# Attention output projection: the first two output blocks summed head by head inside the attention's steps, a third ahead of the last head's part

## The chip, the cores and the metric

The kernel runs on one core of one Trainium2 chip. The metric is the device time of one execution in microseconds (us); of a kernel that was run several times it is the median.

## What is computed

The program is a two-layer transformer block (first part) followed by a second block with a state-space branch and a latent-attention branch. Width 1024, 256 positions, batch 1. The change touches the attention of the first part's second layer and what follows it:

```python
q = rope(rms_norm((h @ w_q[j]).reshape(B, T, N_HEADS, HEAD_DIM), q_norm[j]), cos, sin).transpose(0, 2, 1, 3)
att = moba_attention(q, k_blocks, v_blocks, k_mean)         # 8 heads of 128; 256 positions are one block
y = att.transpose(0, 2, 1, 3).reshape(B, T, D) @ w_o[j]     # output projection, 1024 x 1024
x = x + (1.0 + g)[:, None, :] * y
h = modulate(rms_norm(x, norm_g[layer, 2]), sh, sc)         # input of the feed-forward network behind it
```

Since the sequence is one attention block, each head is a causal softmax attention of 256 queries over 256 keys. The output projection sums over all 8 heads: output block n (128 of the 1024 outputs) is the sum over heads k of `w_o[k, n]` (128 x 128) times head k's result (128 x 256).

## The kernel before

**Number format.** A float32 operand is split into a rounded high part and the rest (`hi` and `lo`, type fp32r). A product is hi*hi + lo*hi + hi*lo. `mm2` (lines 363 and 364) does that with two matmuls: the high weights against both halves of the activation side by side (512 columns), and the low weights against the high half (256 columns). `mm3` (line 356) does it with three of 256 columns.

**The weight stream.** All weights come as tiles of 128 x 1024 float32 (512 KB) in one fixed order, in three pools of 5 buffers (`wraw`, `whi`, `wlo`). SyncE's queue loads a tile (line 215), ScalarE casts it to `whi` (line 229), VectorE subtracts to get `wlo` (line 220). The stream keeps up to 4 split tiles ahead: `Stream.next()` first splits until 4 tiles are ahead, then hands out the oldest; `next(True)` ("hold") hands out the oldest and splits nothing. With `late`, the VectorE halves of new splits are queued in a list that the next call of `next` emits first; where the tile handed out is itself among the new ones, the whole list is emitted at once. An engine's instructions stand in the order in which the Python code emits them. The DMA that refills a raw buffer is emitted behind the VectorE half that frees it.

**The attention** (`attention`). The query projection (`proj_b`) comes first; it leaves three tiles of `w_o` split and waiting. Then a loop over `it` from 1 to 10 runs the heads as a pipeline. In step `it`: `s1a(it)` computes the scores (lines 879 to 882) and their maxima (VectorE, 884 to 889); `s1b(it-1)` the exponentials (ScalarE, line 896) and the division (VectorE, 898 and 900); `s2(it-2)` transposes the probabilities (line 907) and copies them (ScalarE, 909); `s3(it-3)` multiplies with the values (840, 841) and writes the head's result to `oo` (trace name `ohl`), high half by ScalarE (842), low half by VectorE (843). Scores end with head 7 in step 7; steps 8 to 10 only finish heads.

**The output projection** (`proj_a`). Eight output blocks n, one after the other. Each takes one weight tile (all 8 heads of that block): 8 pairs of matmuls on TensorE, one per head, into a PSUM bank with tag A or B in turn. Then `update` (line 558) adds the block, times the gate, to the residual `X` with two VectorE operations, ScalarE squares `X` for the next normalisation (lines 471, 473, 479), and GpSimd adds the squares (484). With each block, `next()` splits the tile four ahead, and a planner (`plan`, `tick`) lets out one of two waiting matrix-vector rows (`gemv`, VectorE, line 389). PSUM has 8 banks: tags A, B, C and D with two each. Tag C is free from step 5 on.

**Behind it.** `st_half` and `st_finish` sum the squares (line 500), take the power -0.5 on GpSimd (520) and spread the result by TensorE (526); `modulated` writes the next input `hhl` (533 to 538), and the next feed-forward network starts on TensorE with line 356.

Of the kernel before, what the change touches and what calls it, by code (L numbers as in the profile page):

```python
# [18 lines left out]
KB = 8  # L19
# [11 lines left out]
W_OUT = (1.2, 1.6, 1.5, 1.6)  # L31
KV_A = 97
AT_A, AT_Q, AT_O = 150, 0, 2
KV_W = [0] * 2 + [1] * 13
SLOTS = 135
CUTS = (0, 0.27, 0.27, 0.6)
# [214 lines left out]
class Kernel:  # L251
# [391 lines left out]
            self.flush()  # L643
            self.st_half(D, gap)

    def proj_a(self, a, evac, kb=KB, tiles=8, tags="AB", late=True, wide=0):
        hi = lo = None
        for n in range(tiles):
            p = self.ps(tags[n % len(tags)])
            mm, w = (self.mm2, 2 * T) if n < wide else (self.mm3, T)  # L650
            for k in range(kb):
                b = n * kb + k
                if b % 8 == 0:
                    hi, lo = self.next(late=late)
                mm(p[:, :w], hi, lo, b % 8, a[:, k], k == 0, k == kb - 1)
            evac(n, p[:, :w])
        self.los()
# [134 lines left out]
    def attention(self, hh, gate_fn, pre):  # L792
        nc, V = self.nc, self.nc.vector
        with self.tc.tile_pool(name="attn", bufs=1) as self.ap:
            self.rope_table(1, "q", 1.0)
            QT = self.ap.tile([128, 8, T], F32, name="QT")
            rq = self.ap.tile([128, 8, 2], F32, name="rq")
            self.shift(self.ap, 192)
            oo = self.ap.tile([128, 8, 2, T], F32R, name="ohl")
            pend = []  # L800

            def evac(nch, pp):
                while pend:
                    pend.pop(0)()
                if nch:
                    last_pp.extend(pp)
                    return
                stats(pp, nch)
                for th in range(2):
                    rope(pp[th], nch, th)  # L810

            def stats(pp, nch):
                for th in range(2):
                    self.qk_stats(pp[th], nch, th, rq)

            def rope(p, nch, th):
                m1 = self.qk_rope(p, nch, th, rq, "q")
                pend.append(lambda: self.qk_transpose(m1, QT, nch, th))
            last_pp = []
            S, P, PT = {}, {}, {}  # L820

            def rest():
                while pend:
                    pend.pop(0)()

            def s1a(h):
                S[h] = self.softmax_a(self.ps("D" if h < 2 else "A"), QT[:, h], self.KT[:, h], 0,
                                      lambda th: rq[:, h, th:th + 1], rq[:, h, :])

            def s1b(h):  # L830
                P[h] = self.softmax_b(*S.pop(h))

            def s2(h):
                PT[h] = self.p_transpose(P.pop(h))

            def s3(h):
                pt = PT.pop(h)
                po = self.ps("D")
                d = slice(h * 128, h * 128 + 128)
                nc.tensor.matmul(po[:, :256], self.VV[:, 0, d], pt[:, :256], start=True, stop=False)  # L840
                nc.tensor.matmul(po[:, 128:256], self.VV[:, 1, d], pt[:, 256:], start=False, stop=True)
                nc.scalar.copy(oo[:, h, 0], po[:, :T])
                V.tensor_sub(oo[:, h, 1], po[:, :T], oo[:, h, 0].bitcast(F32))

            mids = self.gemvs(AT_A, 152)
            first, mids, last = mids[:AT_Q], mids[AT_Q:len(mids) - AT_O], mids[len(mids) - AT_O:]
            self.plan(first, [0] * 3 + [1] * 3)
            self.proj_b(hh, 2, evac, hooks={HQ: rest, (1, 6): lambda: s1a(0)})
            self.drain()
            for it in range(1, 11):  # L850
                if it == 4:
                    rest()
                if it < 8:
                    s1a(it)
                if it - 1 < 8:
                    s1b(it - 1)
                if it == 1:
                    stats(last_pp, 1)
                if 0 <= it - 2 < 8:
                    s2(it - 2)  # L860
                if it < 3:
                    rope(last_pp[it - 1], 1, it - 1)
                if 0 <= it - 3 < 8:
                    s3(it - 3)
                if mids:
                    mids.pop(0)()
            g = gate_fn()
            self.st_begin(KB)

            self.plan(mids + last, [1] * len(mids + last))  # L870
            self.proj_a(oo, lambda n, p: self.update(n, p, g), wide=KB - 1)
            self.drain()
            self.pre = pre()
            self.st_half(D, "g11")
# [66 lines left out]
    def phase1(self):  # L941
# [12 lines left out]
        with ExitStack() as p1:  # L954
# [152 lines left out]
            for l in range(2):  # L1107
# [32 lines left out]
                if l == 0:  # L1140
# [5 lines left out]
                    self.modulated(rbs, self.pre, hh)  # L1146
                    self.plan(self.gemvs(KV_A, 104), KV_W, ssm[2], 16)
                    self.kv_project(hh)
# [800 lines left out]
```

## Time and profile before

| | |
|---|---|
| median of 3 runs | 1303.39 us |
| lowest and highest of the 3 | 1303.30 and 1306.41 us |
| the profiled execution | 1308.08 us |
| its span, first to last instruction | 1306.3 us |
| mean granted TensorE clock in the span | 0.987 of full |
| busy share of the span: TensorE, VectorE, ScalarE, GpSimd | 96%, 78%, 51%, 13% |
| attention's loop of steps, in the profiled execution | from 704.8 to 726.4 us |
| output projection | from 726.4 to about 748.9 us |

The trace is that of the profiled execution, one core. 1.8 us of its time lie outside its span. In the trace, a matmul's duration holds its way through the array, so neighbours overlap: the time that a matmul takes from the engine is read from start to start. A number in square brackets behind a row is the engine's idle time before it and what ended it. PEclk is the granted clock of TensorE: 1.00 is 2.4 GHz, 0.50 is 1.2 GHz.

### The profile page before, as it was taken

How to read it: one execution, taken by the hardware profiler on the slowest of the kernel's cores; microseconds unless marked ns; L12 is line 12 of the kernel's file. 1: busy time of each engine (PE TensorE's matmuls, PEld its weight loads, DVE VectorE, ACT ScalarE, POOL GpSimd, SP SyncE). 2: the span in 40 equal slices, each digit the busy share in tenths (PEclk: the TensorE clock that was granted, in tenths of full speed). 3: DMA queues.
4: the chain of work that ended last, by engine and by line, in shares of the span. 5: the costliest groups of instructions: out<-in, count | busy, mean ns of one | idle time of the engine just before them, and what ended most of it. 6: DMA issues, size and time to landing. Idle time of an engine off the chain costs nothing.

```text
span 1306.3 us, 25415 instructions
## 1 busy us (share of the span) xinstructions
PE 1258.7 (96%) x9870; PEld 1167.4 (89%) x9870; DVE 1015.6 (78%) x1768; ACT 669.4 (51%) x1170; POOL 165.3 (13%) x285
## 2 busy tenths in 40 slices
PE   7999999999999999999998999999999899989998
PEld 5999988899988779999886899998888888989997
DVE  6789896789999789999977777878853576537774
ACT  4455444555444665544447555444465855437443
POOL 1000011100002000121111201000210791100000
PEclk9999999899999999999999999999998999989999
DMA  9899996788899568998974478778655544764852
GB/s 365 297 344 386 335 369 237 251 310 259 274 326 332 203 256 299 312 324 301 360 279 145 129 237 268 265 258 282 223 195 172 156 130 124 226 202 143 292 191 81
DMA packets 119850, 331.14 MB, mean 253 GB/s; under 512 B 28273, under 2 KB 39409, under 8 KB 119666
## 3 DMA queue, kind: packets, MB, share of 16 engines
q1 hardware_dynamic: 119730, 329.52, 73.4%
q8 instruction: 77, 1.26, 0.4%
q14 instruction: 43, 0.35, 0.1%
HBM read 317.94 MB, written 10.49 MB: 251 GB/s over the span
## 4 chain that ended last, share of the span: by engine, by line
PE 71%; DVE 4%; ACT 4%; issue 2%; DMA 2%; POOL 1%; SPq 0%; DVEq 0%; ACTq 0%; POOLq 0%
PE psD L356 13%; PE psB L356 12%; PE psA L356 11%; PE psC L356 7%; PE psA L363 5%; PE psB L363 4%; PE psA L364 3%; PE psB L364 2%; DVE wlo L220 1%; PE psA L368 1%; PE psA L369 1%; PE psA L370 1%; PE psB L368 1%; PE psB L370 1%; PE psB L369 1%
## 5 line engine op out<-in xcount | busy, mean ns | idle before, releaser
L220 DVE TENSOR_TENSOR wlo<-wraw,whi 128x1024 fp32r<-128x1024 f32 x391 | 481.3, 1236 | 44.6 <-ACT whi L229 43.4
L229 ACT CAST whi<-wraw 128x1024 fp32r<-128x1024 f32 x391 | 403.1, 1049 | 94.5 <-ACT whi L229 32.7
L356 PE MATMUL psA<-hhl,whi 128*128 128x256 f32 x960 | 247.4, 283 | 4.7 <-ACT hhl L534 4.6
L356 PE MATMUL psB<-hhl,whi 128*128 128x256 f32 x976 | 248.4, 281 | 0.0
L356 PE MATMUL psD<-hhl,whi 128*128 128x256 f32 x1120 | 213.7, 283 | 0.4 <-ACT hhl L534 0.4
L356 PEld LDWEIGHTS psA<-hhl,whi 128*128 128x128 f32 x960 | 180.2, 189 | 7.9 <-ACT hhl L534 6.2
L356 PEld LDWEIGHTS psB<-hhl,whi 128*128 128x128 f32 x976 | 183.8, 190 | 0.0
L389 DVE SCALAR_TENSOR_TENSOR junk<-graw,cb 128x1024 bf16<-128x1024 f32 x146 | 179.3, 1228 | 5.5 <-DMA cb<-in_c 5.5
L356 PEld LDWEIGHTS psD<-hhl,whi 128*128 128x128 f32 x1120 | 178.6, 190 | 2.7 <-issue 1.8
L356 PE MATMUL psD<-hhl,wlo 128*128 128x256 f32 x560 | 157.2, 281 | 0.0
L356 PE MATMUL psB<-hhl,wlo 128*128 128x256 f32 x488 | 136.9, 281 | 0.0
L356 PE MATMUL psA<-hhl,wlo 128*128 128x256 f32 x480 | 134.9, 281 | 1.3 <-DVE wlo L220 1.3
L363 PE MATMUL psA<-shl,whi 128*128 128x512 f32 x352 | 123.8, 392 | 0.0
L356 PEld LDWEIGHTS psD<-hhl,wlo 128*128 128x128 f32 x560 | 106.3, 190 | 0.0
L364 PE MATMUL psA<-shl,wlo 128*128 128x256 f32 x352 | 99.2, 282 | 0.0
L356 PE MATMUL psC<-hhl,whi 128*128 128x256 f32 x480 | 93.4, 286 | 0.4 <-DVE hhl L1456 0.4
L356 PEld LDWEIGHTS psA<-hhl,wlo 128*128 128x128 f32 x480 | 91.2, 190 | 1.7 <-DVE wlo L220 1.7
L356 PEld LDWEIGHTS psB<-hhl,wlo 128*128 128x128 f32 x488 | 92.4, 189 | 0.0
L363 PE MATMUL psB<-shl,whi 128*128 128x512 f32 x264 | 92.2, 390 | 0.0
L484 POOL TENSOR_TENSOR stacc<-stacc,stsq 128x256 f32<-128x256 f32 x33 | 35.1, 1063 | 381.9 <-ACT stsq L479 340.4
L356 PEld LDWEIGHTS psC<-hhl,whi 128*128 128x128 f32 x480 | 77.0, 191 | 3.2 <-issue 2.2
L363 PEld LDWEIGHTS psA<-shl,whi 128*128 128x128 f32 x352 | 66.1, 188 | 14.3 <-issue 0.8
(453 smaller groups left out, 2362.1 us busy)
## 6 DMA issues: line engine op xcount, KB each, us to landing
wraw<-in_win SPq DMA_DIRECT2D x176, 512.0 KB
graw<-in_ada SPq DMA_DIRECT2D x173, 512.0 KB
wraw<-in_w SPq DMA_DIRECT2D x93, 512.0 KB
wraw<-in_wout SPq DMA_DIRECT2D x88, 512.0 KB
wraw<-in_wkv SPq DMA_DIRECT2D x16, 512.0 KB
hg<-in_ada SPq DMA_DIRECT2D x11, 512.0 KB
Hd<-ct SPq DMA_DIRECT2D x64, 64.0 KB
Gd<-gsb SPq DMA_DIRECT2D x16, 256.0 KB
```

Source lines behind the costliest of these rows:

```text
L220: self.nc.vector.tensor_sub(lo, raw, hi.bitcast(F32))
L229: self.nc.scalar.copy(hi, raw)
L356: self.nc.tensor.matmul(*a, skip_group_check=shared, **kw)
L363: mm(out, hi[:, b], a.rearrange("p x t -> p (x t)"), start=first, stop=False)
L364: mm(out[:, :T], lo[:, b], a[:, 0], start=False, stop=last)
L368: mm(out, ah, whi, start=first, stop=False)
L369: mm(out, ah, wlo, start=False, stop=False)
L370: mm(out, al, whi, start=False, stop=last)
L389: self.nc.vector.scalar_tensor_tensor(junk, self.gemv_tile(j), 1.0, self.cb, op0=OP.mult, op1=OP.mult, accum_out=self.modc[:, j:j + 1])
L484: (eng or nc.gpsimd).tensor_add(acc, acc, sq)
```

## The change

A constant `EARLY = 5` and a helper `early(k)` are added. From step 5 on, each step adds one head's part of output blocks 0 and 1: step `it` adds head `it - 5`, between `s1b` and `s2`, into two PSUM banks of tag C that are kept for the whole sum. So heads 0 to 5 are added in steps 5 to 10. The two weight tiles are taken at step 5 with `next(True)`, the third one, of block 2, after the loop. After the loop TensorE does: head 6 of blocks 0 and 1, heads 0 to 6 of block 2 (tag A), then head 7 of the three blocks. Then the three updates are emitted, and `proj_a` runs with blocks 3 to 7 (`first=3`). The count and the shapes of the matmuls, casts, subtractions and updates stay the same.

```diff
+EARLY = 5
-    def proj_a(self, a, evac, kb=KB, tiles=8, tags="AB", late=True, wide=0):
+    def proj_a(self, a, evac, kb=KB, tiles=8, tags="AB", late=True, wide=0, first=0):
         hi = lo = None
-        for n in range(tiles):
+        for n in range(first, tiles):
...
+            W, E = [], []
+
+            def early(k):
+                if not E:
+                    for _ in range(2):
+                        W.append(self.next(True))
+                        E.append(self.ps("C"))
+                for (hi, lo), p in zip(W, E):
+                    self.mm2(p, hi, lo, k, oo[:, k], k == 0, k == KB - 1)
+
...
                 if it == 1:
                     stats(last_pp, 1)
+                if it >= EARLY:
+                    early(it - EARLY)
                 if 0 <= it - 2 < 8:
                     s2(it - 2)
...
             self.plan(mids + last, [1] * len(mids + last))
-            self.proj_a(oo, lambda n, p: self.update(n, p, g), wide=KB - 1)
+            W.append(self.next(True))
+            p2 = self.ps("A")
+            early(6)
+            E.append(p2)
+            for k in range(KB - 1):
+                self.mm2(p2, *W[2], k, oo[:, k], k == 0, False)
+            early(KB - 1)
+            for n in range(3):
+                self.update(n, E[n], g)
+            self.proj_a(oo, lambda n, p: self.update(n, p, g), wide=KB - 1, first=3)
```

In the changed file the lines lie 1 further down up to the helper (842 is 843 there) and 22 further down behind it (907 is 929). The instructions stand as follows at three places.

TensorE around steps 8 and 9. Before, with buffer numbers (psB holds transposed probabilities, psD a head's result):

```order
L907 MATMUL psB_8911<-k_ident_110,smp_8879 128x128 x3
L840 MATMUL psD_8917<-smpt_8889,VV_104 128x256
L841 MATMUL psD_8917<-smpt_8889,VV_104 128x128
L907 MATMUL psB_8928<-k_ident_110,smp_8905 128x128 x3
L840 MATMUL psD_8934<-smpt_8915,VV_104 128x256
```

TensorE at the same place now (psC_8859 and psC_8860 are output blocks 0 and 1):

```order
L929 MATMUL psB_8925<-k_ident_110,smp_8885 128x128 x3
L841 MATMUL psD_8931<-smpt_8899,VV_104 128x256
L842 MATMUL psD_8931<-smpt_8899,VV_104 128x128
L364 MATMUL psC_8859<-ohl_8520,whi_8643 128x512
L365 MATMUL psC_8859<-ohl_8520,wlo_8644 128x256
L364 MATMUL psC_8860<-ohl_8520,whi_8673 128x512
L365 MATMUL psC_8860<-ohl_8520,wlo_8674 128x256
L929 MATMUL psB_8946<-k_ident_110,smp_8915 128x128 x3
```

Four matmuls of the projection now stand between one head's value product and the next head's transposes.

ScalarE from the last two heads' results into the projection, before (`whi<-wraw` is the cast of a weight tile, `stacc` and `stsq` are squares of the residual):

```order
L842 CAST ohl<-psD 128x256 x2
L229 CAST whi<-wraw 128x1024
L473 ACTIVATE stacc<-X 128x256
L229 CAST whi<-wraw 128x1024
L479 ACTIVATE stsq<-X 128x256
```

ScalarE at the same place now:

```order
L843 CAST ohl<-psD 128x256 x2
L474 ACTIVATE stacc<-X 128x256
L480 ACTIVATE stsq<-X 128x256 x2
L230 CAST whi<-wraw 128x1024 x4
L480 ACTIVATE stsq<-X 128x256
```

The first cast, that of block 3's tile, stood ahead of all squares; now it and the next three casts stand behind the squares of blocks 0, 1 and 2.

VectorE at that place, before (X is the residual):

```order
L389 SCALAR_TENSOR_TENSOR junk,modc<-graw,cb 128x1024
L558 SCALAR_TENSOR_TENSOR X<-psA,gate_8955,X 128x256 x2
L220 TENSOR_TENSOR wlo<-wraw,whi 128x1024
L389 SCALAR_TENSOR_TENSOR junk,modc<-graw,cb 128x1024
L558 SCALAR_TENSOR_TENSOR X<-psB,gate_8955,X 128x256 x2
```

VectorE at that place now:

```order
L559 SCALAR_TENSOR_TENSOR X<-psC,gate_8981,X 128x256 x4
L559 SCALAR_TENSOR_TENSOR X<-psA,gate_8981,X 128x256 x2
L221 TENSOR_TENSOR wlo<-wraw,whi 128x1024 x4
L390 SCALAR_TENSOR_TENSOR junk,modc<-graw,cb 128x1024
L559 SCALAR_TENSOR_TENSOR X<-psB,gate_8981,X 128x256 x2
```

The three updates now stand together ahead of four subtractions, where updates and subtractions took turns; the matrix-vector rows moved behind them.

## Rows read from the trace of the kernel before

**Rows 1.** The page's parts 1, 3 and 4, one line of each.

```profile
PE 1258.7 (96%) x9870; PEld 1167.4 (89%) x9870; DVE 1015.6 (78%) x1768; ACT 669.4 (51%) x1170; POOL 165.3 (13%) x285
...
HBM read 317.94 MB, written 10.49 MB: 251 GB/s over the span
...
PE 71%; DVE 4%; ACT 4%; issue 2%; DMA 2%; POOL 1%; SPq 0%; DVEq 0%; ACTq 0%; POOLq 0%
```

**Rows 2.** Timeline of TensorE: start us, us, engine, line, operation, operands [idle <-releaser].

```profile
466.45 0.50 PE L369 MATMUL psA<-wlo,hhl 128*128 128x512 f32 x1 [1.40 <-DVE wlo L220]
...
718.60 0.39 PE L879 MATMUL psA<-KT,QT 128*128 128x128 f32 x2
...
719.42 0.50 PE L907 MATMUL psB<-k_ident,smp 128*128 128x128 f32 x3
...
720.41 0.39 PE L879 MATMUL psA<-KT,QT 128*128 128x128 f32 x2
...
721.23 0.50 PE L907 MATMUL psB<-k_ident,smp 128*128 128x128 f32 x3
...
722.80 0.61 PE L907 MATMUL psB<-k_ident,smp 128*128 128x128 f32 x3 [0.41 <-DVE smp L900]
...
724.46 0.61 PE L907 MATMUL psB<-k_ident,smp 128*128 128x128 f32 x3 [0.40 <-DVE smp L900]
...
725.70 0.70 PE L840 MATMUL psD<-smpt,VV 128*128 128x256 f32 x2
...
726.37 0.48 PE L363 MATMUL psA<-ohl,whi 128*128 128x512 f32 x1
...
726.81 0.39 PE L363 MATMUL psA<-ohl,whi 128*128 128x512 f32 x1
727.03 0.28 PE L364 MATMUL psA<-ohl,wlo 128*128 128x256 f32 x1
727.15 0.39 PE L363 MATMUL psA<-ohl,whi 128*128 128x512 f32 x1
...
729.12 0.28 PE L364 MATMUL psA<-ohl,wlo 128*128 128x256 f32 x1
```

**Rows 3.** Timeline of ScalarE, first and last blocks of the projection.

```profile
730.47 0.42 ACT L473 ACTIVATE stacc<-X 128x256 f32<-128x256 f32 x1 [2.50 <-DVE X L558]
730.80 1.04 ACT L229 CAST whi<-wraw 128x1024 fp32r<-128x1024 f32 x1
...
749.72 1.03 ACT L229 CAST whi<-wraw 128x1024 fp32r<-128x1024 f32 x1
```

**Rows 4.** Timeline of VectorE, key projection of layer 0 and the output projection.

```profile
465.18 1.22 DVE L220 TENSOR_TENSOR wlo<-wraw,whi 128x1024 fp32r<-128x1024 f32 x1
...
729.44 1.00 DVE L558 SCALAR_TENSOR_TENSOR X<-psA,gate,X 128x256 f32<-128x256 f32 x2 [0.74 <-PE psA L364]
730.36 1.21 DVE L220 TENSOR_TENSOR wlo<-wraw,whi 128x1024 fp32r<-128x1024 f32 x1
...
750.84 1.21 DVE L220 TENSOR_TENSOR wlo<-wraw,whi 128x1024 fp32r<-128x1024 f32 x1
```

**Rows 5.** TensorE's waits over the span: who for whom, total us, times, longest.

```profile
PE psA L1644 <- DMA Tb<-Rd: 4.5, 1, 4.5
...
PE psA L879 <- DVE m L728: 2.2, 1, 2.2
PE psC L500 <- ACT stacc L473: 2.1, 1, 2.1
```

**Rows 6.** Busy time by stretch: length, PE, PEld, DVE, ACT, POOL (instructions), PEclk, DMA share, GB/s.

```profile
710.30:713.70 3.40, 2.60 (x11) 2.44 (x12) 3.29 (x11) 1.95 (x6) 0.00 (x0) 0.52 0.04 17
...
754.80:758.20 3.40, 3.40 (x16) 3.40 (x17) 3.29 (x8) 2.37 (x7) 0.00 (x0) 0.50 0.96 337
976.80:986.90 10.10, 10.10 (x42) 9.12 (x42) 3.90 (x6) 3.69 (x7) 2.29 (x2) 0.50 0.34 104
...
1167.90:1174.70 6.80, 5.66 (x50) 5.31 (x51) 1.76 (x3) 1.59 (x3) 0.00 (x0) 0.50 0.22 80
```

## The prediction

> **What bounds the kernel now.** I read the page first: TensorE is busy for 96% of the span and carries 71% of the chain that ended last, VectorE and ScalarE 4% each [rows 1]. So time is won where TensorE waits, and lost wherever something new makes it wait. Then I read the place itself in TensorE's timeline [rows 2]. In the middle of the loop a step takes 720.41 - 718.60 = 1.81 us from score to score without a wait; its tail, from the transposes to the next step's first instruction, takes 720.41 - 719.42 = 0.99. In steps 8 to 10 there are no scores, the tail is all the work, and it takes longer: from the transposes at 721.23 to those at 722.80, to those at 724.46, to the value product at 725.70, which is 1.57, 1.66 and 1.24 us, 4.47 in all against 3 x 0.99 = 2.97. **1.5 us are waits** for the division of the softmax (the releaser is line 900). Third, the projection: its pairs of matmuls follow each other every 727.15 - 726.81 = 0.34 us, 2.8 us for a block of 8. It does not wait for weights, since ScalarE's cast of a tile stands ahead of the squares that wait for the updates.
>
> **The fill.** The change adds no arithmetic. It moves 12 pairs (heads 0 to 5, two blocks), 12 x 0.34 = 4.1 us of TensorE's work, from behind the loop into steps 5 to 10. In steps 5 to 7 TensorE is full, so the steps grow by 0.7 us each and nothing is won there. In steps 8 to 10 the two pairs of a step (0.69 us) stand where the waits of 0.58, 0.67 and 0.25 us were (the three times above less 0.99), and cover them. The chain through head 7 still fits: from its scores to its transposes TensorE now has three times two pairs and two tails, 3 x 0.69 + 2 x 0.99 = 4.05 us, where the chain needed about 3.2 before (724.46 - 721.23). Each entry into such a pair from the attention's matmuls can cost up to 0.1 us (726.37 to 726.81 is 0.44, against 0.34 for the next pair), on six entries 0 to 0.6; part of this is the end of the matmul before it, so I take 0.2. The fill is worth **-1.3 us**, bounds -1.5 and -0.9.
>
> **The new wait.** ScalarE's and VectorE's programs are where it goes wrong. Block 3's tile was cast ahead of every square; now its cast stands behind the squares of blocks 0, 1 and 2, and these wait for updates which wait for head 7 of those blocks. The three tiles taken with "hold" split nothing in the meantime. That ScalarE doesn't pass a waiting square shows in [rows 3]: the square at 730.47 ends 2.50 us of idling, and the cast at 730.80, whose data needed no update, comes only behind it. Queued behind the squares are four casts; for the first of them TensorE waits. Let T be the time at which TensorE has issued head 7 of block 2. Block 0's last pair is issued two pairs earlier, at T - 0.69. An update starts 0.32 us after the start of its block's last matmul (729.12 [rows 2], 729.44 [rows 4]), which is 0.2 after that matmul's issue is over (727.15 - 727.03 = 0.12 for one): the first one at T - 0.48. Updates follow each other every 730.36 - 729.44 = 0.92 us and last 1.00 [rows 4], so the third ends at T - 0.48 + 1.84 + 1.00 = T + 2.36. The square starts 0.03 later (730.44 to 730.47), the cast 0.33 behind it, and takes 1.04 [rows 3]: the high weights are there at T + 3.76. The subtraction starts 0.09 behind a cast (749.72 + 1.03 to 750.84) and takes 1.22; TensorE goes on 0.05 after one (465.18 + 1.22 to 466.45 [rows 2, 4]). That is T + 5.1. Of this TensorE fills 0.22 with the one matmul that needs the high weights alone. **+4.9 us**, all on the path, since nothing else stands in TensorE's queue. Bounds 4.5 and 5.3, for four handovers read to a tenth.
>
> What follows of it is off the path. VectorE has four subtractions, two matrix-vector rows (1.2 us each, like a subtraction) and two updates to catch up on, while a block takes TensorE 2.8 us; it is level by block 5. The next network's first four weight loads now leave SyncE's queue together, behind these subtractions. Four times 512 KB at 251 GB/s [rows 1] is 8.4 us, the first one 2.1; they start at T + 5 and the first cast of them is due two blocks later, after T + 10. The matrix-vector loads queued behind them are for rows much later. GpSimd's five middle additions only shift. I cost all this at nothing; if a load were late, ScalarE's next squares would wait for it, by up to 2 us.
>
> **The clock.** Every wait of TensorE of 2.1 us or more behind the start-up [rows 5] is followed by a stretch at 1.2 instead of 2.4 GHz. Behind the 4.5 us wait the low clock lasts from 1167.9 to 1174.7 with TensorE at work for 5.66 us of it; at half speed that work costs 2.8 us. Behind the 2.2 us wait it lasts 3.4 us with 2.60 at work: 1.3 us. Another stretch, 754.8 to 758.2, costs 1.7. The longest, 10.1 us behind a 2.1 us wait, costs 5.05 [rows 6]. So the low level costs 1.3 to 5. My wait is nearest to the one of 4.5, but for one matmul in it; I take a value between the two nearest in cost, **+2.2 us**. The Trainium skill (TensorE: Matmul & The Clock Gate, section Terms) puts the penalty at the throttled time times the share of pulses withheld. By it the stretch of 6.8 us would cost 3.4, and the sum would be 1.2 higher; the trace doesn't agree, since 1.1 us of that stretch pass while TensorE still waits.
>
> **Sum.** -1.3 + 4.9 + 2.2 = +5.8 us. The profiled execution would go from 1308.08 to 1313.9. It is 4.7 us above the median of the runs, and nothing in the sum belongs to that excess; so I put the sum on the median: 1303.39 + 5.8 = **1309.2 us**. Behind the projection the program is the same, each stage waits for the one before it, and TensorE is full, so the delay stays. The forecast's own range, with a fill of -1.5 to -0.9, a wait of 4.5 to 5.3 and a clock cost of 1.3 to 5, is 1307.7 to 1312.8.
>
> **Rivals.**
> Fill alone: the wait is hidden, and only -1.3 counts, 1302.1 us. The loop waits and the projection doesn't, which speaks for mixing them. Against it stands ScalarE's order: the cast would have to pass three squares. It decides if block 3's low weights were there by T, five microseconds earlier than the rows allow. Chance 0.05. The Trainium skill (Perfetto Trace Analysis, Optimization Strategy) says that where the busiest engine changes over time, interleaving such regimes can help; by that rule alone the time would be this one. The trace bears out the 1.5 us of gaps that it would fill, and not that their filling is free here.
> The clock falls otherwise further on, the case that ends on the other side, not slower. The stretch at 976.8 [rows 6] hangs on a wait of 2.1 us, the shortest that is followed by the low clock; arriving 6 us later it might not be. That is worth -5.05, the sum +0.75, 1304.1 us. It decides if that wait passes at full clock. Against it: the median lies 4.7 us below the profiled execution, about the price of this stretch, so the median may be without it already. Chance 0.1.
> The clock stays up or costs under 0.9 us behind the new wait: about +3.6, 1307.0 us. Chance 0.1; no wait of this length in the trace got off so.
> The delay costs more: a new long stretch at the low clock, or a late weight load, +9 to +12, 1312.4 to 1315.4 us. For it, the 10.1 us stretch that one 2.1 us wait left; against it, that wait was followed by more short ones. Chance 0.1.
>
> **How the numbers follow.** The forecast has 0.65. What a measurement can tell from no change is about 0.3%, 3.9 us, so the line is at 1307.3. Above it lie the forecast and the dear case: 0.75. Within 0.3%: fill alone, the other clock, the cheap clock, 0.25 less 0.03 for the first two together (-6.3 us): 0.22. Faster 0.03. The range of 8 in 10 has to take in one of the cases below the forecast's own; it reaches from 1304.0, just under the other clock's 1304.1, to 1312.8, where the dear case begins, and leaves out fill alone and the dear case, 0.15.
>
> **What would show it.** Right, in the changed kernel's trace: TensorE without waits in steps 8 to 10 [rows 2]; a wait of 3.6 to 4 us at the first matmul of block 3, released by ScalarE's line 230, and one of about 1 us at the second, released by VectorE's line 221; three updates in a row, then square, then cast; a granted clock of 0.50 for 3 to 7 us behind it; the projection's end some 6 us later against the loop's start at step 5. Wrong: block 3 starting on block 2's heels, which would mean that the cast came earlier than the order says; or the delay gone by the end of the span, which would mean slack further on that the page's 96% doesn't show.

## The result, and the profile after

| | before | changed |
|---|---|---|
| median, same chip | 1303.35 us (6 runs) | 1310.07 us (6 runs) |
| lowest and highest | 1301.05 and 1306.41 us | 1307.70 and 1314.48 us |
| the profiled execution | 1308.08 us | 1309.61 us |
| its span | 1306.3 us | 1307.8 us |

The ratio is 1.0055, 95% interval 1.0034 to 1.0076: slower by 4 to 10 us. The sum of the prediction was +5.8 us.

The totals of the page hardly moved, as before in [rows 1]:

```profile
PE 1258.5 (96%) x9870; PEld 1166.6 (89%) x9870; DVE 1015.4 (78%) x1768; ACT 669.9 (51%) x1170; POOL 166.3 (13%) x285
...
PE 71%; DVE 4%; ACT 4%; issue 2%; DMA 2%; POOL 1%; SPq 0%; DVEq 0%; ACTq 0%; POOLq 0%
```

The change shows only at its place. TensorE's timeline of the changed kernel, against [rows 2] (line 901 is a score, 929 a transpose, 364 and 365 the projection's pairs):

```profile
717.48 0.39 PE L901 MATMUL psA<-KT,QT 128*128 128x128 f32 x2
...
720.04 0.39 PE L901 MATMUL psA<-KT,QT 128*128 128x128 f32 x2
...
725.87 0.49 PE L929 MATMUL psB<-k_ident,smp 128*128 128x128 f32 x3
...
727.55 0.49 PE L929 MATMUL psB<-k_ident,smp 128*128 128x128 f32 x3
...
733.93 0.28 PE L365 MATMUL psA<-ohl,wlo 128*128 128x256 f32 x1
737.83 0.58 PE L364 MATMUL psB<-ohl,whi 128*128 128x512 f32 x1 [3.61 <-ACT whi L230]
739.09 0.58 PE L365 MATMUL psB<-ohl,wlo 128*128 128x256 f32 x1 [0.68 <-DVE wlo L221]
739.46 0.63 PE L364 MATMUL psB<-ohl,whi 128*128 128x512 f32 x1
739.89 0.41 PE L365 MATMUL psB<-ohl,wlo 128*128 128x256 f32 x1
```

Steps 8 to 10 have no waits any more (1.68 us from transposes to transposes, no bracket). Then block 3's first matmul waits 3.61 us for the high weights, its second 0.68 us for the low ones, and in the next pair the second matmul starts 0.43 us behind the first (739.89 - 739.46) where it was 0.22 (727.03 - 726.81 in [rows 2]): the low clock.

What TensorE waits for stands in ScalarE's timeline, against [rows 3]:

```profile
734.60 0.42 ACT L474 ACTIVATE stacc<-X 128x256 f32<-128x256 f32 x1 [4.14 <-DVE X L559]
735.51 0.42 ACT L480 ACTIVATE stsq<-X 128x256 f32<-128x256 f32 x1 [0.50 <-DVE X L559]
736.42 0.42 ACT L480 ACTIVATE stsq<-X 128x256 f32<-128x256 f32 x1 [0.50 <-DVE X L559]
736.75 3.87 ACT L230 CAST whi<-wraw 128x1024 fp32r<-128x1024 f32 x4
```

and in VectorE's, against [rows 4]:

```profile
733.56 1.92 DVE L559 SCALAR_TENSOR_TENSOR X<-psC,gate,X 128x256 f32<-128x256 f32 x4 [2.57 <-PE psC L365]
735.39 1.00 DVE L559 SCALAR_TENSOR_TENSOR X<-psA,gate,X 128x256 f32<-128x256 f32 x2
737.80 4.63 DVE L221 TENSOR_TENSOR wlo<-wraw,whi 128x1024 fp32r<-128x1024 f32 x4 [1.42 <-ACT whi L230]
```

ScalarE idles 4.14 us in front of a square, with four casts queued behind it that need no update; then update, square, update, square, update, square, cast.

I measure the place from the first score of step 5 to the last matmul of block 7, "the stretch". TensorE's timeline of the kernel before (step 5, block 3, the last matmul of block 7, the next network), then the end in the changed one:

```profile
716.79 0.39 PE L879 MATMUL psA<-KT,QT 128*128 128x128 f32 x2
...
734.78 0.39 PE L363 MATMUL psB<-ohl,whi 128*128 128x512 f32 x1
...
748.56 0.28 PE L356 MATMUL psB<-ohl,whi 128*128 128x256 f32 x1
...
754.21 0.38 PE L356 MATMUL psA<-hhl,whi 128*128 128x256 f32 x1 [0.35 <-ACT hhl L534]
```

```profile
755.41 0.28 PE L357 MATMUL psB<-ohl,whi 128*128 128x256 f32 x1
...
761.06 0.38 PE L357 MATMUL psA<-hhl,whi 128*128 128x256 f32 x1 [0.35 <-ACT hhl L535]
```

Before it lasts from 716.79 to 748.56 = 31.77 us, now from 717.48 to 755.41 = 37.93: **+6.16 us**. Behind it nothing changed: from block 7's last matmul to the next network's first one it is 5.65 us in both (748.56 to 754.21, 755.41 to 761.06).

The two profiled spans differ by only 1.5 us all the same. How the changed kernel makes up for most of its delay can be read at two waits that both kernels have. TensorE's timeline of the kernel before, and of the changed one:

```profile
976.74 1.01 PE L500 MATMUL psC<-ones,stacc 128*128 128x1 f32 x4 [2.09 <-ACT stacc L473]
...
1169.04 0.65 PE L1644 MATMUL psA<-Tb,U 128*32 128x128 f32 x8 [4.55 <-DMA Tb<-Rd]
```

```profile
981.68 0.61 PE L501 MATMUL psC<-ones,stacc 128*128 128x1 f32 x4 [2.10 <-ACT stacc L474]
...
1171.52 0.64 PE L1666 MATMUL psA<-Tb,U 128*32 128x128 f32 x8 [4.55 <-DMA Tb<-Rd]
```

The changed kernel is 4.9 us behind at the first, 2.5 at the second. Its stretches at the low clock from 700 us on (columns as in [rows 6]):

```profile
710.90:714.30 3.40, 2.85 (x12) 2.10 (x11) 3.29 (x11) 1.57 (x5) 0.00 (x0) 0.51 0.00 0
738.10:744.90 6.80, 6.12 (x19) 5.04 (x19) 6.16 (x8) 2.52 (x3) 0.00 (x0) 0.50 0.63 205
983.90:987.30 3.40, 3.40 (x18) 3.40 (x18) 1.31 (x2) 1.64 (x3) 1.24 (x1) 0.50 0.34 136
1018.40:1021.80 3.40, 3.40 (x20) 3.40 (x19) 0.00 (x0) 2.81 (x5) 1.04 (x4) 0.56 0.38 74
1171.50:1174.90 3.40, 3.38 (x39) 3.02 (x40) 0.42 (x1) 1.41 (x3) 0.00 (x0) 0.51 0.44 152
```

I call TensorE's busy time in such a stretch, times one less the granted clock, the lost work. The new stretch at 738.1 has 6.12 x 0.50 = 3.1 us of it. But those behind the projection have 1.70 + 1.50 + 1.66 = 4.9 us where the three of before [rows 6] have 1.70 + 5.05 + 2.83 = 9.6. With the 0.7 us by which step 5 began later, 0.7 + 6.2 - 4.7 = 2.2 us should be left, and 1.5 is. The waits ahead of the stretches at 976 and 1168 us are the same in both kernels, so this is the scatter of one execution (more of it below), and the medians carry the verdict.

### The profile page after: what moved, and what is told of

It reads as the page before. It is cut to its first block, busy times and chain, and to the rows that moved or that the text cites. A ratio compares the mean times of both kernels' runs of the same rounds, so it can differ in the third digit from the quotient of the medians.

```text
span 1307.8 us, 25414 instructions
## 1 busy us (share of the span) xinstructions
PE 1258.5 (96%) x9870; PEld 1166.6 (89%) x9870; DVE 1015.4 (78%) x1768; ACT 669.9 (51%) x1170; POOL 166.3 (13%) x285
## 4 chain that ended last, share of the span: by engine, by line
PE 71%; DVE 4%; ACT 4%; issue 2%; DMA 2%; POOL 1%; SPq 0%; DVEq 0%; ACTq 0%; POOLq 0%
PE psD L357 13%; PE psB L357 12%; PE psA L357 12%; PE psC L357 7%; PE psA L364 5%; PE psB L364 4%; PE psA L365 2%; PE psB L365 2%; DVE wlo L221 1%; PE psA L369 1%; PE psA L370 1%; PE psA L371 1%; PE psB L370 1%; PE psB L371 1%; PE psB L369 1%
## 5 line engine op out<-in xcount | busy, mean ns | idle before, releaser
L596 ACT CAST shl<-sf 128x256 fp32r<-128x256 f32 x88 | 35.8, 407 | 84.1 <-DVE sf L594 84.1
```

Of the source, the lines that this page charges most:

```text
L596: nc.scalar.copy(ss[:, i, 0], s)
```

## The experiments

The theory: the order of the queues, ScalarE's above all, makes the wait, +4.9 us; the fill of steps 8 to 10 is real, -1.4; the low clock behind the wait is the rest. Rivals: the three blocks in PSUM or the sums within the steps cost something by themselves, or the fill is worth nothing. Each kernel was run beside the kernel before on the same chip. The ratio is an estimate from all runs of both kernels and need not be the quotient of the two medians. "Stretch" is as above, 31.77 us before; "to the network" is from the first score of step 5 to the first matmul of the network behind, 37.42 us before and 43.58 in the changed kernel.

| kernel | median (runs) | before | ratio, 95% interval | stretch | to the network |
|---|---|---|---|---|---|
| x1_cast_first | 1304.96 (12) | 1305.12 | 1.0007 (0.9993 to 1.0020) | 30.77 | 36.95 |
| x2_hold_only | 1309.36 (12) | 1305.12 | 1.0033 (1.0017 to 1.0048) | 37.94 | 43.60 |
| x3_fill_wait | 1307.53 (12) | 1305.12 | 1.0018 (1.0006 to 1.0030) | 35.26 | 40.91 |
| x4_two_blocks | 1307.56 (12) | 1305.12 | 1.0018 (1.0006 to 1.0030) | 34.69 | 40.35 |
| x5_cast_in_steps | 1304.57 (12) | 1305.03 | 1.0001 (0.9989 to 1.0013) | 30.33 | 38.16 |
| x6_steps_8_10 | 1304.68 (1) | 1305.03 | | 30.48 | 37.10 |
| x7_busy_waits | 1299.88 (7) | 1305.03 | 0.9964 (0.9951 to 0.9978) | 30.33 | 38.17 |
| x8_rows_early | 1304.12 (10) | 1304.78 | 0.9995 (0.9982 to 1.0007) | 30.36 | 36.01 |
| x9_both | 1298.20 (5) | 1304.78 | 0.9938 (0.9915 to 0.9961) | 30.37 | 36.47 |
| x10_busy_alone | 1299.84 (8) | 1304.78 | 0.9959 (0.9943 to 0.9976) | 31.77 | 37.42 |

The stretches came out within what was expected, or 0.1 us from it, but for x6_steps_8_10 (30.48 where 30.8 was expected). The times tell less. x1_cast_first, x5_cast_in_steps and x8_rows_early were expected 0.6 to 1.5 us below the kernel before, and none can be told from it. x2_hold_only was expected 5 to 6.5 us above and came 4.2 above (interval 2.2 to 6.3), x3_fill_wait 3.4 and came 2.4 above (0.8 to 3.9).

**The casts ahead of the squares.** The changed kernel with one line more: the tiles of blocks 3 and 4 are split before the updates. `split` emits both halves, so the two casts stand ahead of ScalarE's squares and the two subtractions ahead of VectorE's updates.

```diff
             W.append(self.next(True))
+            self.ws.split(self.ws.nh + 2)
             p2 = self.ps("A")
```

> The changed kernel with one line more: behind the loop of steps, ahead of the three updates, the tiles of blocks 3 and 4 are split (cast by ScalarE, subtraction by VectorE). The early sums stay as they are. Measure: the stretch from the first score matmul of step 5 to the last matmul of block 7, 31.8 us before the change, 37.9 in the changed kernel. My theory (the casts' place behind the squares makes the wait, and the wait brings the low clock): no wait at block 3, clock 1.00, stretch 30.4 us plus at most 0.8 for a short wait at block 5, whose subtraction stands behind a matrix-vector row and an update; time 0.6 to 1.4 us below the kernel before. Rival (the sums in the steps cost more than they fill, by switching TensorE between two kinds of work): the stretch stays above 34 us and the time 3 us or more above before. Second rival (the weight loads of the next network come late): block 3 runs without a wait, but the squares wait on later casts and the stretch stays above 33.

All waits of TensorE between steps 8 and the network in this kernel:

```profile
737.44 0.38 PE L365 MATMUL psB<-ohl,wlo 128*128 128x256 f32 x1 [0.16 <-DVE wlo L221]
746.99 0.61 PE L501 MATMUL psC<-ones,stacc 128*128 128x1 f32 x4 [0.61 <-POOL stacc L485]
750.18 0.43 PE L527 MATMUL psC<-k_ident,strs 128*128 128x128 f32 x2 [1.39 <-POOL strs L521]
751.73 0.38 PE L357 MATMUL psA<-hhl,whi 128*128 128x256 f32 x1 [0.36 <-ACT hhl L535]
```

The two waits at block 3 are gone (0.16 us is left at block 5), the clock stays at 1.00 through the projection, and the stretch is 1.0 us shorter than before. One added line takes back all that the change costs: the order of the queues is the cause. It moved ScalarE's casts and VectorE's subtractions together, so it doesn't show that ScalarE's order alone makes the wait, and the changed kernel's trace speaks against that: its third update ends at 735.39 + 1.00 = 736.39, and then VectorE idles 1.42 us for the cast. Earlier casts alone would have saved about these 1.4 us. By this estimate some 3.4 of the 4.8 us that block 3's second matmul comes late (739.09, against 734.05 + 0.22) would stay, since the subtraction stands behind three updates. No run moved the casts alone. Half of the gain is lost again at 746.99, a new wait for GpSimd's sum of squares.

**The held tiles alone.** No sums within the steps; blocks 0 to 2 stand behind the loop, whole, and their updates together behind them.

```diff
-                if it >= EARLY:
-                    early(it - EARLY)
...
-            W.append(self.next(True))
...
+            for n in range(3):
+                W.append(self.next(True))
+                E.append(self.ps("AB"[n % 2]))
+                for k in range(KB):
+                    self.mm2(E[n], *W[n], k, oo[:, k], k == 0, k == KB - 1)
```

> No sums in the steps: blocks 0, 1 and 2 are computed one after the other behind the loop, as before the change, but their three tiles are taken with hold, and their three updates are emitted together behind block 2, as in the changed kernel. So only the order of casts, squares and updates differs from the kernel before. My theory: updates 0 and 1 are done during blocks 1 and 2; from the end of block 2 it is 0.2 + 1.0 (update) + 0.03 + 0.33 + 1.04 (cast) + 0.09 + 1.22 (subtraction) + 0.05 = 4.0 us to the second matmul of block 3, 3.7 us lost, and 1.3 to 2.8 by the clock. Stretch 31.8 + 5 to 6.5 = 36.8 to 38.3 us, time 5 to 6.5 us above before. Rival (the loss comes with the sums in the steps): stretch 31.8, time as before.

```profile
734.72 0.80 PE L364 MATMUL psB<-ohl,whi 128*128 128x512 f32 x1 [2.48 <-ACT whi L230]
735.98 0.58 PE L365 MATMUL psB<-ohl,wlo 128*128 128x256 f32 x1 [0.47 <-DVE wlo L221]
```

The wait comes without any sum in the steps. It is shorter, 2.95 against 4.29 us, since the updates of blocks 0 and 1 run while TensorE is still at blocks 1 and 2. The lost work is 3.0 us, so 2.95 + 3.0 is about 5.9 of the 6.17 us by which the stretch grows.

**The wait filled with dead work.** The changed kernel with 16 dead matmuls, whose result nothing reads, in front of block 3.

```diff
             early(KB - 1)
+            pd = self.ps("D")
+            for _ in range(16):
+                nc.tensor.matmul(pd, W[2][0][:, 0], oo[:, 0].rearrange("p x t -> p (x t)"), start=True, stop=True)
```

> The changed kernel with 16 matmuls of 512 columns more, into a free PSUM bank that nothing reads, right behind head 7 of block 2: 16 x 0.22 = 3.6 us of TensorE's wait are filled with work. My theory (wait 4.8 us and clock 2.8 us add up): the second matmul of block 3 still comes 5.0 us behind the end of block 2, the granted clock stays 1.00 from step 5 to block 7, the stretch is 31.8 - 1.4 + 4.8 = 35.2 us, 2.7 below the changed kernel, and the time about 3.4 us above the kernel before. Rival (the low clock costs nothing here, the whole 7.6 us is wait for weights): stretch 37.9 as in the changed kernel.

TensorE's timeline, and a window over the rest of the projection (columns as in [rows 6]):

```profile
732.02 3.89 PE L893 MATMUL psD<-ohl,whi 128*128 128x512 f32 x16
735.80 0.50 PE L364 MATMUL psB<-ohl,whi 128*128 128x512 f32 x1
737.06 0.38 PE L365 MATMUL psB<-ohl,wlo 128*128 128x256 f32 x1 [0.76 <-DVE wlo L221]
```

```profile
733.00:748.50 15.50, 14.74 (x81) 12.42 (x80) 13.40 (x20) 8.79 (x12) 4.71 (x5) 1.00 0.65 229
```

Block 3 starts 735.80 - 732.02 = 3.78 us behind block 2, exactly as in the changed kernel (733.93 + 0.12 to 737.83), so the dead work delays nothing. The clock stays at 1.00. The stretch is 35.26 us, 2.67 shorter than in the changed kernel. That separates the terms: **fill -1.4, wait +4.9, clock +2.7**, together 6.2.

**Two blocks.** Only blocks 0 and 1 go ahead, block 2 runs as before, `first=2`.

```diff
-            W.append(self.next(True))
-            p2 = self.ps("A")
             early(6)
...
-            for n in range(3):
+            for n in range(2):
                 self.update(n, E[n], g)
```

> Only blocks 0 and 1 are summed in the steps; head 6 and 7 of them and their updates follow the loop, and block 2 runs as before the change, from its tile that is split already. The casts of blocks 3 to 5 then stand behind two squares and run while TensorE computes block 2; but the subtractions stand behind the update of block 2. My theory: from block 2's end 0.2 + 1.0 (update) + 1.22 (subtraction) + 0.05 = 2.5 us to the second matmul of block 3, 2.2 lost; the clock may drop or not (0 to 2.8 us). Stretch 31.8 - 1.4 + 2.2 = 32.6 us, up to 35.4 with the low clock; time 0.8 to 3.6 us above before. Rival (the third block's sum alone makes the loss): stretch 30.4, time 1.4 below before.

```profile
728.53 0.50 PE L364 MATMUL psC<-ohl,whi 128*128 128x512 f32 x1 [0.22 <-DVE ohl L844]
732.55 0.50 PE L364 MATMUL psB<-ohl,whi 128*128 128x512 f32 x1 [0.27 <-ACT whi L230]
734.51 0.38 PE L365 MATMUL psB<-ohl,wlo 128*128 128x256 f32 x1 [1.46 <-DVE wlo L221]
```

Without the third held tile, 1.95 us of waiting is left; a low stretch of 3.4 us behind it has 1.7 us of lost work, and the stretch is +2.9. Most of that waiting, 1.46 us, is for a subtraction that stands behind an update; the cast is late by only 0.27. So VectorE's order makes a wait by itself. The third block makes the loss more than twice as large, but two blocks already lose.

**The casts within the steps.** The changed kernel, with the tiles of blocks 3 and 4 cast and subtracted at the end of steps 9 and 10, and the two matrix-vector rows two blocks later.

```diff
+                if it >= 9:
+                    self.ws.split(self.ws.ns + 1)
...
-            self.plan(mids + last, [1] * len(mids + last))
+            self.plan(mids + last, [0, 0, 1, 1])
```

> The changed kernel with the tiles of blocks 3 and 4 split in steps 9 and 10, where ScalarE and VectorE have gaps, and with the two matrix-vector rows two blocks later, behind the subtraction that block 5 needs. Stretch from step 5's first score matmul to block 7's last matmul: 31.8 us before the change, 30.8 with the casts behind the loop (0.16 us of wait at block 5). My theory: no wait left in the projection, clock 1.00, stretch 31.8 - 1.4 = 30.4 us; time 1 to 1.5 us below the kernel before, which the interval can hardly tell from no change. Rival (the casts delay the softmax of head 7 in steps 9 and 10): a wait returns there and the stretch is 31 us or more.

The stretch is 30.33 us without a single wait: the whole fill, -1.44. But the network behind starts 0.7 us later than before. TensorE's new wait, GpSimd's last additions of squares, and one of the two matrix-vector rows on VectorE:

```profile
749.41 0.60 PE L501 MATMUL psC<-ones,stacc 128*128 128x1 f32 x4 [1.82 <-POOL stacc L485]
```

```profile
744.55 1.08 POOL L485 TENSOR_TENSOR stacc<-stacc,stsq 128x256 f32<-128x256 f32 x1 [2.66 <-ACT stsq L480]
748.29 1.06 POOL L485 TENSOR_TENSOR stacc<-stacc,stsq 128x256 f32<-128x256 f32 x1 [2.66 <-ACT stsq L480]
```

```profile
744.95 1.77 DVE L390 SCALAR_TENSOR_TENSOR junk<-graw,cb 128x1024 bf16<-128x1024 f32 x1
```

The additions come 3.74 us apart where blocks follow each other every 2.8. VectorE does a subtraction and a matrix-vector row between two updates there, and the last update, square and sum are late. The row takes 1.77 us where such rows take 1.22 in the kernel before; one of GpSimd's additions falls into its time. From the projection to the network it is 38.16 - 30.33 = 7.83 us instead of 5.65: the 1.82 us and the low clock behind it (3.1 us of lost work, part of it past the network's start) give the gain back.

**Three heads in steps 8 to 10.** The kernel x1_cast_first with the sums starting at step 8 instead of 5.

```diff
-EARLY = 5
+EARLY = 8
...
-            early(6)
+            for k in range(11 - EARLY, KB - 1):
+                early(k)
```

> As the kernel with the casts behind the loop, but with EARLY = 8: only heads 0 to 2 are summed in the steps, one in each of steps 8 to 10; heads 3 to 7 follow the loop. My theory (the gain is the filling of the waits of steps 8 to 10, and the sums in steps 5 to 7 win nothing): steps 5 to 7 take 1.81 us each as before the change, no wait in steps 8 to 10, stretch 30.8 us as with EARLY = 5. Rival (the longer steps 5 to 7 are needed, since they let VectorE and ScalarE get ahead): waits of 0.2 to 0.6 us return in steps 8 and 9, stretch 31.2 us or more.

The stretch is 30.48 us, 0.29 less than with six heads (30.77 in x1_cast_first), and no wait is left in the projection: the pairs in steps 5 to 7 win nothing, as the prediction said. Steps 5 to 7 are back at 1.81 us each. A wait of 0.60 us for GpSimd's sum stays.

**The rows earlier.** The kernel x5_cast_in_steps with the two matrix-vector rows at the end of steps 8 and 9, and the subtractions behind head 7's result.

```diff
+                if it in (8, 9):
+                    last.pop(0)()
                 if it >= 9:
-                    self.ws.split(self.ws.ns + 1)
+                    self.ws.split(self.ws.ns + 1, lo)
+            while lo:
+                lo.pop(0)()
...
-            self.plan(mids + last, [0, 0, 1, 1])
+            self.plan(mids + last, [])
```

> As the casts within the steps (blocks 3 and 4 cast in steps 9 and 10), with VectorE's two matrix-vector rows moved out of the projection's last blocks into steps 8 and 9, and the subtractions of tiles 3 and 4 behind head 7's result. Theory (the 1.4 us won up to the projection's end are lost behind it because VectorE and with it GpSimd's last sums of squares come late): from step 5 to block 7's end 30.4 us as before this edit, no wait for GpSimd's sum or one under 0.7 us where 1.82 stood, and from step 5 to the next network's first matmul 36.0 to 36.8 us against 37.42 in the kernel before; median 0.6 to 1.4 us below the kernel before, about what can be told. Rival (the end of that chain, squares, GpSimd, power, is as long whatever VectorE does before): 37.4 or more, median unchanged.

```profile
747.97 0.61 PE L501 MATMUL psC<-ones,stacc 128*128 128x1 f32 x4
...
752.87 0.38 PE L357 MATMUL psA<-hhl,whi 128*128 128x256 f32 x1 [0.35 <-ACT hhl L535]
```

The wait for the sum is gone, and the network starts 752.87 - 716.86 = 36.01 us behind step 5: the fill's 1.4 us arrive there in full. So VectorE's load was what took them in x5_cast_in_steps: the rows, since the two subtractions that were moved with them were over before the first update in both kernels (which starts at 732.51 and 732.95). The rival (a chain that is as long whatever VectorE does) falls. In the median they can't be told: 0.9995, interval 0.9982 to 1.0007, holds both -1.4 us and nothing.

**TensorE kept at work through waits.** 32 dead matmuls at three places where TensorE waits and the low clock follows: 8 in front of the scores of step 3, 8 in front of the 256-wide norm's sum, 16 within the wait of 4.5 us. First on x5_cast_in_steps:

> The kernel with the casts in steps 9 and 10, and with matmuls that nothing reads (512 columns, 0.22 us each, free PSUM bank) in three waits of TensorE that every kernel here has: 8 ahead of the scores of step 3 (wait of 2.2 us), 8 ahead of the first sum of squares of the second block's latents (2.1 us), 16 ahead of the seventh output chunk of the state-space branch, which waits for a load (4.5 us). The waits' ends don't move, since they hang on VectorE, ScalarE and a load. My theory (the price of a wait is in good part the low clock behind it): the low stretches behind these three waits, 1.4 to 1.6, 1.7 to 5.1 and 1.6 to 3.0 us of lost work in the kernels so far, are gone, and the time is 4.5 to 9 us below the kernel before. Rival (the low clock has nothing to do with what TensorE does in the wait, or other waits keep it low): stretches and time as without them.

then on x8_rows_early, and on the kernel before:

```diff
+    def busy(self, tag, n, w, a):
+        p = self.ps(tag)
+        for _ in range(n):
+            self.nc.tensor.matmul(p, w, a, start=True, stop=True)
...
+                if it == 3:
+                    hi = self.ws.split_t[self.ws.nh][0]
+                    self.busy("D", 8, hi[:, 0], flat(hi[:, :4]))
...
+        if dim == 256 and self.h2 is not None:
+            self.busy("C", 8, self.h2[:, 0, 0, :128], flat(self.h2[:, 0]))
...
+                if ch == 6:
+                    self.busy("B", 16, hh[:, 0, 0, :128], flat(hh[:, 0]))
```

> The kernel of the run above with the same dead matmuls as the earlier run with busy waits: 8 of 512 columns ahead of the scores of step 3, 8 ahead of the sum of squares in the state-space block's 256-wide norm, 16 at the seventh chunk behind the 4.5 us wait. They add 32 matmuls whose results nobody reads. If the two effects add, the time is that of the earlier run with busy waits, 1299.9, less what the run above gains, so 1298.5 to 1299.9 us and faster than the kernel before by 0.3 to 0.5%; low clock only at about 235 us and perhaps behind the projection.

> The kernel before, with the same 32 dead matmuls at the same three places and nothing else changed. It tells what the clock alone gives. Theory (the low stretches at 710, 976 and 1168 us go when TensorE works through those waits, worth 1.45, 5.0 and 2.8 us in the profiled execution of before, less where the median run has a shorter one): median 1299 to 1301.5 us, stretch from step 5 to block 7's end 31.8 us as before. Rival (the gain of the earlier run came from the early sums): median 1303 to 1306, as the kernel before.

Windows of the kernel before with the dead matmuls, over the three places (columns as in [rows 6], where the clock is 0.52, 0.50 and 0.50 there):

```profile
708.00:718.00 10.00, 7.94 (x54) 6.42 (x54) 9.12 (x34) 7.15 (x22) 0.17 (x1) 1.00 0.11 43
960.00:990.00 30.00, 28.91 (x258) 25.59 (x256) 13.21 (x19) 23.37 (x36) 2.98 (x3) 1.00 0.56 180
1155.00:1180.00 25.00, 23.43 (x228) 21.83 (x227) 13.42 (x24) 15.05 (x29) 0.00 (x0) 1.00 0.37 114
```

The three low stretches are gone, and these matmuls, the only change, are worth 4.9 us (1304.78 to 1299.84, interval 3.1 to 7.4). The mean granted clock of the eight runs is 0.992 to 0.997, against 0.987 to 0.991 in the eighteen of the kernel before. The early sums are worth nothing that can be told in x7_busy_waits (0.9964, against 0.9959 without them on another chip). x9_both is the fastest, 1298.20 us, 6.6 below the kernel before and a little below its expectation. Against x10_busy_alone that is 1.6 us, about the fill, but the intervals of the two overlap. What each of the three places is worth was not tried apart.

## Why the prediction was right, point by point

**The fill** was put at -1.3 us (bounds -1.5 and -0.9). From step 5 to the moment at which block 3 is due it was 734.78 - 716.79 = 17.99 us before (line 363's first matmul into block 3 starts at 734.78) and is 734.05 - 717.48 = 16.57 now: -1.42. (734.05 is the last matmul ahead of block 3, 733.93, and its 0.12 us.) Steps 5 to 7 take 2.56 us (720.04 - 717.48), 0.06 more than 1.81 + 0.69: three entries at 0.06 are the 0.2 us of the text. Steps 8 to 10 take 1.68 us, 0.99 + 0.69 to the hundredth. The tenth that was won beyond -1.3 lies at head 7: from the first matmul of its value product to the projection it was 726.37 - 725.70 = 0.67 us before and is 729.80 - 729.23 = 0.57 now. One reading of the text is off: the last 0.25 of the 1.5 us of waits, ahead of 725.70, ended with ScalarE's copy of the probabilities and not with the division; the term is the same. That steps 5 to 7 win nothing is shown by x6_steps_8_10.

**The wait.** With T = 734.05, the forecast had the first update at T - 0.48, the third's end at T + 2.36, block 3's first matmul at T + 3.76 and its second at T + 5.1. Measured: T - 0.49, T + 2.34, T + 3.78, T + 5.04. A chain of handovers, each read off a row of before, holds to a few hundredths. The term, +4.9, measured 4.9 where x3_fill_wait has it alone (35.26 less x8_rows_early's 30.36). x1_cast_first shows the cause: casts ahead of squares and subtractions ahead of updates, no wait. The text named both engines' programs but followed the chain through ScalarE; by the estimate above, VectorE's updates alone would have kept most of the wait.

**The clock** was put at +2.2 us, between the rows for 1.3 and for 2.8; it is 2.7 by x3_fill_wait, 3.1 as lost work at 738.1. The term is undersized by half a microsecond. The wait of 4.5 us, which the text named as nearest, was the better row than a value between two. The Trainium skill's product (TensorE: Matmul & The Clock Gate, section Terms) would give 6.8 x 0.5 = 3.4, an estimate; the trace has TensorE at work for 6.12 us of the 6.80, and 2.7 is what the end of the projection shows.

**Nothing behind it** held: no wait of TensorE follows at blocks 4 to 7, no weight load is late, and 5.65 us lie between projection and network as before. The delay reaches the end: the medians differ by 6.7 us. The interval, 4 to 10 us, is too wide to bear out the sum's terms; that rests on the traces of the place.

**The sum on one execution** was the weak step. For the profiled execution it said 1313.9, and 1309.61 came. Low stretches that had nothing to do with the change were shorter by 4.7 us in that execution. The rival "the clock falls otherwise further on" happened in it, but not for its reason: the wait of 2.1 us is still there. The sentence that every wait of 2.1 us or more is followed by the low clock is wrong as a rule; in x5_cast_in_steps the same 2.10 us at 976.26 was followed by none. Nor is 2.1 us the shortest, as that rival has it: ahead of the stretch at 754.8 stands a wait of 1.43 us, at 752.66. Setting the sum on the median was right.

**The other rivals.** "Clock stays up" (1307.0) is what x3_fill_wait makes happen: 2.4 us above the kernel before on its chip, where the rival had +3.6 (interval 0.8 to 3.9). "Fill alone" (1302.1) is what x8_rows_early makes happen at the place: 1.4 us less, at the price of three more moves. The Trainium skill's advice to interleave stages with different limits (Perfetto Trace Analysis, Optimization Strategy) bears out at the place, not in the median, and only when the other engines' queues are reordered with it. "Delay costs more" didn't come.

## What to carry to other kernels

Work that is moved on one engine moves its partners in the in-order queues of the others: ask of each instruction that now stands in front (here three squares on ScalarE and three updates on VectorE) what is queued behind it that needed nothing of it (here four casts and their four subtractions), and emit that first, on every engine that has a part in it. A wait of some microseconds on TensorE costs more than itself: here 4.9 us of waiting and 2.7 us at half clock, for 1.4 us of filled gaps. Where a wait can't be removed, dead matmuls in it can be the cheaper cure.

## What the runs showed of the hardware

The same waits are followed by low stretches of very different length. Lost work in us by place, from windows of 1 us in each profiled execution:

| kernel | 237 us | 709 | projection | 754 | 976 | 1014 | 1168 | sum |
|---|---|---|---|---|---|---|---|---|
| before | 3.0 | 1.5 | | 1.7 | 5.0 | | 2.8 | 14.0 |
| changed | 3.0 | 1.4 | 3.1 | | 1.7 | 1.7 | 1.6 | 12.5 |
| x1_cast_first | 1.7 | 1.6 | | 1.7 | 5.0 | | 2.8 | 12.7 |
| x2_hold_only | 1.7 | 1.7 | 3.0 | 1.7 | 5.1 | | 3.0 | 16.1 |
| x3_fill_wait | 1.7 | 1.6 | | | 1.7 | 1.7 | 2.4 | 9.1 |
| x4_two_blocks | 1.6 | 1.6 | 1.7 | 1.6 | 3.4 | 1.7 | 2.4 | 14.0 |
| x5_cast_in_steps | 2.9 | 1.6 | | 3.1 | | | 2.5 | 10.0 |
| x6_steps_8_10 | | 1.5 | | 2.9 | 3.4 | 1.7 | 1.7 | 11.3 |
| x7_busy_waits | 2.9 | | | 3.1 | | | | 6.0 |
| x8_rows_early | 2.9 | 3.0 | | 1.7 | 3.4 | 1.7 | 1.7 | 14.4 |
| x9_both | 3.1 | | | 1.5 | | | | 4.6 |
| x10_busy_alone | 1.6 | | | | | 1.6 | | 3.2 |

The wait ahead of the place at 976 is 2.09 or 2.10 us in all kernels without dead matmuls there, and the stretch behind it loses 0 to 5.1 us. The wait that was followed by none, in x5_cast_in_steps:

```profile
976.26 0.61 PE L501 MATMUL psC<-ones,stacc 128*128 128x1 f32 x4 [2.10 <-ACT stacc L474]
```

So one profiled execution tells the price of a wait in clock only to a few microseconds. At 237 and 754 us the low clock comes with shorter waits, 1.20 us (at 236.78) and 1.43 (at 752.66) in the kernel before. Whether the runs lie closer with the waits filled is not shown: x10_busy_alone's eight span 3.9 us, but x8_rows_early's ten, with the waits as they were, span 3.1.

Taking the lost work off does not explain all of the scatter: 1308.08 - 14.0 is 1294.1 us for before, 1303.85 - 14.4 is 1289.5 for x8_rows_early, 4.6 less where 1.4 was won. Most of the other 3 us can be found by following the same matmul through both traces. x8_rows_early is 0.95 us ahead at the scores of step 3 already (708.22 against 709.17), ahead of all its changes. And at 1014 us its 1.7 us of lost work delay it by 0.4 us only: from the matmul at 1001.67 to that at 1021.00 it is 19.33 us before, from 998.54 to 1018.28 it is 19.74, in part since two waits for ScalarE of 0.43 and 0.86 us give way to one of 0.40. So lost work can overstate what a stretch costs, where part of it falls into time that the engine would have waited. About a microsecond is left open.
